# A decoder trunk on one core: one room 64 bytes longer, banks by name, output weights split in two

## Chip, cores and metric

The kernel runs on one NeuronCore of a Trainium2 chip. The metric is the device time of one execution in microseconds (us). Before the change it is 1954.59 us, the median of three runs (1953.89 to 1954.96). In the views the engines are called PE (TensorE matmul), PEld (TensorE weight load), DVE (VectorE), ACT (ScalarE), POOL (GpSimd) and SP (SyncE, which issues most DMAs).

## What is computed

A trunk of two layers on 1024 tokens of width 1024, in float32. Cut to what matters:

```python
for i in range(2):
    h = rmsnorm(x, norm_mixer[i])
    mix = short_conv_mixer(h, ...) if i == 0 else swa_sink_attention(h, ...)
    x = x + mix
    h = rmsnorm(x, norm_ffn[i])
    g, u = split(h @ w_gate_up[i])        # 1024 x 5632
    x = x + (silu(g) * u) @ w_down[i]     # 2816 x 1024
```

The attention has 16 query heads and 4 key and value heads of 64, a window of 128 tokens worked off in blocks of 128, a distance bias, a sink column in the softmax, and a norm of queries and keys per head. Its output goes through an output matrix `attn_w_o` (1024 x 1024), which the kernel calls `w_o`.

## The kernel before

**Precision.** Each matrix product is made of three float32r products: every operand is split into a high part (a rounding copy) and a low part (what the copy left over), and high x high, high x low and low x high are added in a PSUM bank. A weight block of 128 x 128 so gives three matmuls of 512 columns. For a channel mixer granule these are L918, L919 and L921, for the output matrix L1025, L1026 and L1027, for the projections to queries, keys and values L1590, L1591 and L1592, and for the first products of the convolution L157 and L161. The split is a copy on ScalarE (L857, `act.copy`) and a subtraction on VectorE (L858).

**Schemes of seven products.** The big products (gate, up and down, and most of the convolution's input product) are done by a scheme of seven products instead of eight (`sums_of`, `KINDS = 7`), in granules of up to four weight blocks (`ring_granule`). A granule's split weights go to a room of a ring of eight rooms with the tags G0 to G7, the next one free each time; 13 us (`LEAD`) before the matmuls are due, its copy is placed.

**Order.** All work from the convolution's end on is written out by a planner, `Line`. `line.work(n, f)` appends n matmuls to TensorE's order and moves the planned time on by n x `MM` = n x 0.2265 us; `line.at(t, f)` places other engines' work at a planned time. Nothing waits for a planned time: it only sets the order in which each engine, and each DMA queue, gets its instructions; each engine then works them off in order, as fast as its operands come.

**Rooms.** SBUF rooms are given out by tag with `slot`, in the order of the first request: the constants, XS0 to XS7 and A0 to A5 (8,192 bytes in each partition), two each of WR, WH and WL (4,096), then G0 to G11 (4,096 each, but G2, which has 32 bytes more, because attention lays two sets of 4 x 129 exponents in it), s0 and s1 (2,048), X0 to X7 (4,096) and small ones. PSUM has eight banks: four with the tags acc0 to acc3 and P0 to P3. A tag's next user waits until the last one's readers are done.

**Attention** (`attention_layer`). Its lead-in (L1917 and on) has three parts that matter here:

- Projections. `kv_piece(b, k)` and `q_piece(m, k)` add the k-th of eight steps of the key and value product of token block b, and of one half of the query product of block m // 2. A product's bank comes from `product_bank`, which goes round P0, P1, P2 in the order of first use. Readers of a key and value bank are `kv_v_hi`, `kv_v_lo`, `kv_square` and, last, `kv_scale` (L1683); of a query bank `q_square` and, last, `q_scale` (L1747).
- Units u = 0 to 31, one for each block and group of heads, some 6.7 us each in the plan: `scores` (L1797), then on VectorE `merge` (L1807), `bias` (L1814) and `least` (L1827), on ScalarE `exponents` (L1833), on GpSimd `normal` (L1842); a unit later `turn` (L1848, TensorE transposes the weights), `turn_hi`, `turn_lo`, `select` (L1864, GpSimd); two units later `values` (L1883). In between TensorE gets pieces of projections from `fill`, one (`next_piece`) ahead of `turn` and five behind. `key_turn` (L1696) and `q_turn` (L1762) transpose keys and queries into bank P3; `key_hi` and `key_lo` (L1700 on ScalarE, L1705 on VectorE) read the one, `q_keep` (L1767, ScalarE) the other. `q_lo` (L1756) and `o_lo` (L1914) are work of GpSimd.
- From unit 24 on the pieces are those of the output product for the first half of the tokens (`tail_piece`, `tail_part`, `tail_item`), 64 of them: eight weight tiles m of eight steps. Two more rounds, u = 32 and 33, finish the last turn and the last values, and what is left of the 64 follows. `tail_weights(m, t)` places the work for tile m, due at t: the load (L113) at t - 14.0, the copy of all 1024 columns on ScalarE at t - 5.2, the subtraction on VectorE at t - 4.2. Tile m adds up in bank P0 or P1 (`m % 2`), and is added to X on VectorE (L1050) and squared on ScalarE (L1042, L1048).

The same `tail_weights` serves the first layer and the second half of the tokens.

Of the kernel before, what the change touches and what calls it, by code (L numbers as in the profile page):

```python
# [13 lines left out]
ALU = mybir.AluOpType  # L14

P = 128
D = 1024
# [52 lines left out]
def trunk_kernel(ctx: ExitStack, tc: tile.TileContext, xT, small, table, w_in, w_out, w_kv, w_q, w_o, w_gu, w_dn, out):  # L70
# [7 lines left out]
    def slot(tag, shape=(P, D), dtype=F32, bufs=1):  # L78
        uid[0] += 1
        return sb.tile(list(shape), dtype, tag=tag, name=f"{tag}_{uid[0]}", bufs=bufs)  # L80
# [11 lines left out]
    def plain(ap):  # L92
        return ap.bitcast(F32)
# [111 lines left out]
    for tag in ("WR", "WH", "WL"):  # L205
        slot(tag, bufs=2)
    for tag in [f"G{k}" for k in range(12)]:
        slot(tag, (P, D + 8) if tag == "G2" else (P, D))
    for tag in ("s0", "s1"):
        slot(tag, (P, HALF))  # L210
    X = [slot(f"X{k}") for k in range(NK)]
# [766 lines left out]
    def channel_mixer(layer, next_stage, src_of, operands, raw_tags, extra_tags, slots, line, lead_in):  # L978
# [9 lines left out]
        ring_granule, bank_at = tools.ring_granule, tools.bank_at  # L988


        def tail_weights(m, t):
            it = {}
            c = slice(0, n_op * P)

            def load():
                it["w"] = Weights()
                it["w"].load(src_of(m), 0, n_op)

            def hi():
                it["w"].alloc()  # L1000
                it["steps"] = split_steps(it["w"].hi[:, c], it["w"].lo[:, c], it["w"].raw[:, c])
                it["steps"][0]()

            at(t - 14.0, load)
            at(t - 5.2, hi)
            at(t - 4.2, lambda: it["steps"][1]())
            return lambda: (it["w"].hi, it["w"].lo)

        tails = {}
# [1 line left out]
        def tail_part(h, m, ks):  # L1011

            c = slice(h * HALF, h * HALF + HALF)
            if (h, m) not in tails:
                tag = f"P{m % 2}" if layer and h == 0 else "acc"
                tails[h, m] = tail_weights(m, line.end), bank_at(("tail", h, m), "x", tag)
            w, get = tails[h, m]
            for k in ks:

                def three(k=k):  # L1020
                    hi, lo = w()
                    xs = operands[k]
                    ps = get()
                    kc = slice(k * P, (k + 1) * P)
                    pe.matmul(ps, hi[:, kc], xs[:, 0, c], start=k == 0, stop=False, skip_group_check=True)  # L1025
                    pe.matmul(ps, hi[:, kc], xs[:, 1, c], start=False, stop=False, skip_group_check=True)  # L1026
                    pe.matmul(ps, lo[:, kc], xs[:, 0, c], start=False, stop=k == n_op - 1, skip_group_check=True)  # L1027

                line.work(3, three)
# [455 lines left out]
    def attention_layer(line, mixer):  # L1485
        at = line.at
        xs = mixer.xs
        end0 = line.end
        small_mm = 0.42
        small_turn = 0.42  # L1490

# [81 lines left out]


        kv_ps, q_ps = {}, {}
        product_tags = deque(("P0", "P1", "P2"))

        def product_bank():
            tag = product_tags.popleft()
            product_tags.append(tag)  # L1580
            return bank(tag)

        def piece(ps_of, b, k, w):

            def three():
# [7 lines left out]

            line.work(3, three)

        def get_bank(d, key):
            def get():
                if key not in d:
                    d[key] = product_bank()
                return d[key]  # L1600

            return get

        def kv_piece(b, k):
            piece(get_bank(kv_ps, b), b, k, lambda: (WKV[k][:, 0], WKV[k][:, 1]))

        def q_piece(m, k):
            c = slice((m % 2) * HALF, (m % 2 + 1) * HALF)
            piece(get_bank(q_ps, m), m // 2, k, lambda: (WQ[k][0][:, c], WQ[k][1][:, c]))


        def mean_rows(d, b, n):
# [77 lines left out]
        KT = {}  # L1690

        def key_turn(b, c):
            ps = KT[b, c] = bank("P3")
            for g in (0, 1):
                k = kd_room()[:, 2 * c + g].rearrange("p e d -> p (e d)")
                pe.transpose(ps[:, g * P : (g + 1) * P], k, ident)  # L1696
# [59 lines left out]
            pool.tensor_tensor(s[:, :, 1, :], QC[m]["q"], s[:, :, 0, :], ALU.subtract)  # L1756

        def q_turn(m, g):
            ps = QC[m]["ps"] = bank("P3")
            s = QC[m]["split"]  # L1760
            for i in range(QUAD):
                pe.transpose(ps[:, i * P : (i + 1) * P], s[:, QUAD * g + i].rearrange("p e d -> p (e d)"), ident)  # L1762
# [5 lines left out]


        S = {}  # L1770
        sc_tags = [acc_tags[0], acc_tags[1]]
        pt_tag, pv_tag = acc_tags[2], acc_tags[3]
        NU = 2 * 2 * NB

        def parts(u):
# [2 lines left out]

        def e_room(u):
            if "E" not in room:  # L1780
                room["E"] = slot("G2", (P, D + 8))[:, 0 : 2 * QUAD * (P + 1)].rearrange(
                    "p (i h c) -> p i h c", i=2, h=QUAD
                )
            return room["E"][:, u % 2]
# [132 lines left out]
        def lead_in(tail_part, tail_item):  # L1917
# [78 lines left out]
            def unit(u, last):  # L1996

                s = line.end
                begins.append(s)
                n, g = u // 2, u % 2  # L2000
                b, c = n // 2, n % 2
                todo = deque(fill[u] if u < NU else [])

                def next_piece():
                    if todo:
                        f, *args = todo.popleft()
                        f(*args)
                    elif u >= NU:
                        tail_piece()

                if u < NU:
                    line.work(8 * (small_mm + (0.12 if b else 0.0)), scores, u)
                    e = line.end
                    at(s + 0.3, sink, u)
                    for j in (0, 1):
                        if b:
                            at(e + 0.05 + 0.85 * j, merge, u, j)
                        at(e + 0.5 + 0.85 * j, bias, u, j)
                    if b == 0:
                        at(e + 1.5, blank, u)  # L2020
                    at(e + 1.8, least, u)
                    at(e + 2.65, exponents, u)
                    at(e + 4.75, inverse, u)
                    at(e + 5.0, normal, u)
                    if g == 0:
                        kb = (b, 1) if c == 0 else (b + 1, 0)
                        if 0 < kb[0] < NB:
                            turn_keys(*kb, e + 0.3, e + 2.4)
                if 0 <= u - 2 < NU:
                    pb = (u - 2) // 4  # L2030
                    line.work(4 if pb else 2, values, u - 2)
                    at(line.end + 0.05, o_copy, u - 2)
                    at(max(line.end + 0.7, s + 3.6), o_add, u - 2)
                    if g == 1:
                        at(s + 6.95, o_hi, n - 1)
                        at(s + 7.9, o_lo, n - 1)
                next_piece()
                if 0 <= u - 1 < NU:
                    line.work(4 * small_turn, turn, u - 1)
                    at(line.end + 0.05, turn_hi, u - 1)  # L2040
                    at(max(line.end + 0.7, s + 4.2), turn_lo, u - 1)
                    if u - 1 >= 4:
                        at(line.end + 0.75, select, u - 1, 0)
                        at(max(line.end + 1.4, s + 4.95), select, u - 1, 1)
                if u >= NU:
                    for _ in range(6):
                        next_piece()
                    return
                for i in range(5):
                    next_piece()  # L2050
                    if i == (1 if g == 0 else 0) and n + 1 < 16:
                        turn_query(n + 1, g, s + 5.8)
                if n + 2 < 16 and g == 0:
                    m = n + 2
                    for d, f in (
                        (5.75, q_square),
                        (6.35, q_sum),
                        (7.2, q_guess),
                        (6.8 + 3.4, q_newton),
                        (6.8 + 5.2, q_scale),  # L2060
                        (6.8 + 6.2, q_hi),
                        (6.8 + 7.3, q_lo),
                    ):
                        at(s + d, f, m)
                if g == 1 and n < 12 and n % 2:
                    kb = n // 2 + 2
                    for d, f in (
                        (3.57, kv_v_hi),
                        (5.0, kv_v_lo),
                        (5.7, kv_square),  # L2070
                        (6.1, kv_sum),
                        (6.9, kv_guess),
                        (6.8 + 3.5, kv_scale),
                    ):
                        at(s + d, f, kb)
                if g == 0 and c == 1 and b + 1 < NB:
                    at(s + 3.5, dv_sum, b + 1)
                    at(s + 8.0, dv_hi, b + 1)
                    at(s + 8.4, dv_lo, b + 1)
# [129 lines left out]
```

## Time and profile before

| | |
|---|---|
| median of 3 runs | 1954.59 us (1953.89 to 1954.96) |
| the profiled execution | 1954.33 us, its span 1952.6 us |
| mean granted TensorE clock | 0.999 |
| instructions in the span | 24622 |
| HBM traffic | 228.76 MB read, 94.90 MB written |

Where the stages lie in the span: the first products of the convolution up to 52 us, the convolution in granules to about 241, the first layer's output product to 334, its channel mixer to about 975, attention with the first half of its output product from 978 to 1261, the second half to 1306, the second channel mixer to the end.

How to read the views: a row of the timeline is the start in us from the span's start, the duration, engine, line, operation, tiles written and read (buffer numbers left out, so G3 and G7 are both G), shapes and count; in brackets is the engine's idle time before it and what ended that. Durations of matmuls overlap and their ends are modelled; the distance between two starts is the pace. A row of waits is: who waited, for what, us in total, how often, the longest.

### The profile page before, as it was taken

The page shows a single profiled execution, that of the slowest core. Times are in us where ns is not written, and L with a number is a line of the kernel's source. Part 1 is how long each engine was busy: PE and PEld are TensorE (multiplying, and loading weights), DVE is VectorE, ACT ScalarE, POOL GpSimd, SP SyncE. Part 2 cuts the span into 40 slices and gives each one's busy share as a digit, 9 for nine tenths or more (in the row PEclk, how much of TensorE's full clock was granted, in tenths as well). Part 3 has the DMA queues.
Part 4 walks back from the last instruction along what each step waited for, and adds up shares of the span by engine and source line. Part 5 has one row for each costly group of instructions (what it writes and reads, how often), then busy time and mean ns, then how long its engine had stood idle before and what let it go on. Part 6 is the DMA issues. An engine that isn't in the chain of part 4 may idle for free.

```text
span 1952.6 us, 24622 instructions
## 1 busy us (share of the span) xinstructions
PE 1935.1 (99%) x8681; PEld 1580.7 (81%) x8681; DVE 1384.0 (71%) x2357; ACT 855.7 (44%) x1703; POOL 280.6 (14%) x442
## 2 busy tenths in 40 slices
PE   9999999999999999999999998999999999999999
PEld 7888888888888888888888887787888888888887
DVE  8997777876676767665768878678767776765543
ACT  5543444533333334444656766546333333344441
POOL 0000011011111111000025665400111111110000
PEclk9999999999999999999999999999999999999999
DMA  8522185245545537986710003433445554487562
GB/s 314 164 97 81 60 296 199 73 153 185 183 168 198 178 125 275 342 296 211 231 53 1 1 23 130 141 118 119 164 162 171 204 173 168 153 280 257 196 222 99
DMA packets 146764, 325.28 MB, mean 167 GB/s; under 512 B 14288, under 2 KB 54352, under 8 KB 146512
## 3 DMA queue, kind: packets, MB, share of 16 engines
q1 hardware_dynamic: 122592, 239.26, 36.2%
q0 software_dynamic: 23904, 84.42, 12.0%
q8 instruction: 68, 1.11, 0.2%
q14 instruction: 56, 0.46, 0.1%
q10 hardware_dynamic: 144, 0.03, 0.0%
HBM read 228.76 MB, written 94.90 MB: 166 GB/s over the span
## 4 chain that ended last, share of the span: by engine, by line
PE 94%; DVE 3%; ACT 1%; issue 1%; POOL 0%; DMA 0%; SPq 0%; DVEq 0%; POOLq 0%; ACTq 0%
PE acc L921 16%; PE acc L918 16%; PE acc L919 16%; PE P L921 9%; PE P L918 9%; PE P L919 9%; PE acc L1027 2%; PE acc L1025 2%; PE acc L1026 2%; PE P L1590 2%; PE P L1592 2%; PE P L1591 2%; PE acc L1797 1%; PE acc L157 1%; PE acc L1883 1%
## 5 line engine op out<-in xcount | busy, mean ns | idle before, releaser
L921 PE MATMUL acc<-XS,G 128*128 128x512 f32 x880 | 346.6, 394 | 0.0
L918 PE MATMUL acc<-XS,G 128*128 128x512 f32 x880 | 346.1, 393 | 0.0
L919 PE MATMUL acc<-XS,G 128*128 128x512 f32 x880 | 345.9, 393 | 0.0
L919 PEld LDWEIGHTS acc<-XS,G 128*128 128x128 f32 x880 | 165.3, 188 | 38.5
L921 PEld LDWEIGHTS acc<-XS,G 128*128 128x128 f32 x880 | 165.2, 188 | 38.0
L918 PEld LDWEIGHTS acc<-XS,G 128*128 128x128 f32 x880 | 165.3, 188 | 37.9
L918 PE MATMUL P<-A,G 128*128 128x512 f32 x476 | 187.1, 393 | 0.6 <-DVE G L1234 0.6
L921 PE MATMUL P<-A,G 128*128 128x512 f32 x476 | 187.4, 394 | 0.0
L919 PE MATMUL P<-A,G 128*128 128x512 f32 x476 | 187.0, 393 | 0.0
L921 PE MATMUL acc<-A,G 128*128 128x512 f32 x440 | 173.4, 394 | 0.0
L918 PE MATMUL acc<-A,G 128*128 128x512 f32 x440 | 173.2, 394 | 0.0
L919 PE MATMUL acc<-A,G 128*128 128x512 f32 x440 | 173.0, 393 | 0.0
L858 DVE TENSOR_TENSOR G<-WL,G 128x512 fp32r<-128x512 f32 x168 | 114.9, 685 | 56.6 <-ACT G L857 56.6
L857 ACT CAST G<-WR 128x512 fp32r<-128x512 f32 (+1 forms) x200 | 121.0, 605 | 67.1 <-PE acc L921 36.8
L858 DVE TENSOR_TENSOR G<-WR,G 128x512 fp32r<-128x512 f32 (+1 forms) x200 | 133.3, 666 | 12.0 <-ACT G L857 11.2
L857 ACT CAST G<-WH 128x512 fp32r<-128x512 f32 (+1 forms) x158 | 94.8, 600 | 87.3 <-PE acc L921 46.5
L1196 ACT ACTIVATE G<-G 128x512 f32<-128x512 f32 x88 | 55.7, 633 | 165.9 <-DVE G L1267 161.8
L921 PE MATMUL P<-XS,G 128*128 128x512 f32 x316 | 124.4, 394 | 0.0
L919 PE MATMUL P<-XS,G 128*128 128x512 f32 x316 | 124.2, 393 | 0.0
L918 PE MATMUL P<-XS,G 128*128 128x512 f32 x316 | 124.2, 393 | 0.0
L857 ACT CAST G<-WL 128x512 fp32r<-128x512 f32 x168 | 103.5, 616 | 36.0 <-DVE WL L801 31.9
L858 DVE TENSOR_TENSOR G<-WH,G 128x512 fp32r<-128x512 f32 (+1 forms) x158 | 104.4, 661 | 5.4 <-ACT G L857 5.1
(297 smaller groups left out, 3837.4 us busy)
## 6 DMA issues: line engine op xcount, KB each, us to landing
G<-h SPq DMA_DIRECT2D x70, 512.0 KB, 5.1
h<-X POOLq DMA_DIRECT2D x44, 512.0 KB, 5.2
X<-in_w_dn SPq DMA_DIRECT2D x80, 256.0 KB, 3.4
s<-X POOLq DMA_DIRECT2D x40, 512.0 KB, 4.7
WR<-in_w_gu SPq DMA_DIRECT2D x36, 512.0 KB, 6.0
WH<-in_w_gu SPq DMA_DIRECT2D x36, 512.0 KB, 6.2
h<-X POOLq DMA_DIRECT2D x66, 256.0 KB, 3.9
WR<-s SPq DMA_DIRECT2D x54, 256.0 KB, 3.3
```

Of the source, the lines that this page charges most:

```text
L857: lambda: act.copy(out_hi, raw),
L858: lambda: lo_eng.tensor_tensor(out_lo, raw, plain(out_hi), ALU.subtract),
L918: pe.matmul(ps, w[:, 0, c], x[:, 0, :], start=start and e == 0, stop=False, skip_group_check=True)
L919: pe.matmul(ps, w[:, 0, c], x[:, 1, :], start=False, stop=False, skip_group_check=True)
L921: pe.matmul(ps, w[:, 1, c], x[:, 0, :], start=False, stop=last, skip_group_check=True)
L1025: pe.matmul(ps, hi[:, kc], xs[:, 0, c], start=k == 0, stop=False, skip_group_check=True)
L1026: pe.matmul(ps, hi[:, kc], xs[:, 1, c], start=False, stop=False, skip_group_check=True)
L1027: pe.matmul(ps, lo[:, kc], xs[:, 0, c], start=False, stop=k == n_op - 1, skip_group_check=True)
L1196: state["silu"] = act.activation(x, x, AF.Silu)
L1590: pe.matmul(ps, x[:, 0, t], hi, start=k == 0, stop=False)
L1591: pe.matmul(ps, x[:, 0, t], lo, start=False, stop=False)
L1592: pe.matmul(ps, x[:, 1, t], hi, start=False, stop=k == NK - 1)
```

## The change

Four edits, none of which changes a number that is computed:

- The room G2 is 64 bytes longer than 4,096 instead of 32 (in the two places that name its shape). The exponents use as much of it as before.
- Banks of projections are assigned by name: key and value products of block b get P0 or P1 by `b % 2`, even query products P2, odd ones P0 or P1 by `m // 2 % 2`. The second key turn of the lead-in (b = 0, c = 1) gets the bank of `values`, the second query turn (m = 0, g = 1) the bank of `turn`, both among the acc banks, instead of P3. The tails of the first half take P0, P2, P1 in turn.
- For layer 1, first half, tiles 0 to 4 (`early`), the load, the copy on ScalarE and the subtraction are placed earlier, at t - 17.0, t - 8.2, and the subtraction in two pieces of 512 columns at t - 5.6 and t - 3.9.
- In round u = 32 three pieces go ahead of the last turn instead of one.

```diff
-        slot(tag, (P, D + 8) if tag == "G2" else (P, D))
+        slot(tag, (P, D + 16) if tag == "G2" else (P, D))
...
-        def tail_weights(m, t):
+        def tail_weights(h, m, t):
             it = {}
             c = slice(0, n_op * P)
+            early = layer == 1 and h == 0 and m < 5
...
+            def lo(i):
+                h = slice(i * n_op * P // 2, (i + 1) * n_op * P // 2)
+                w = it["w"]
+                dve.tensor_tensor(w.lo[:, h], w.raw[:, h], plain(w.hi)[:, h], ALU.subtract)
+
-            at(t - 14.0, load)
-            at(t - 5.2, hi)
-            at(t - 4.2, lambda: it["steps"][1]())
+            at(t - (17.0 if early else 14.0), load)
+            at(t - (8.2 if early else 5.2), hi)
+            if early:
+                at(t - 5.6, lo, 0)
+                at(t - 3.9, lo, 1)
+            else:
+                at(t - 4.2, lambda: it["steps"][1]())
...
-                tag = f"P{m % 2}" if layer and h == 0 else "acc"
-                tails[h, m] = tail_weights(m, line.end), bank_at(("tail", h, m), "x", tag)
+                tag = ("P0", "P2", "P1")[m % 3] if layer and h == 0 else "acc"
+                tails[h, m] = tail_weights(h, m, line.end), bank_at(("tail", h, m), "x", tag)
...
-            piece(get_bank(kv_ps, b), b, k, lambda: (WKV[k][:, 0], WKV[k][:, 1]))
+            piece(get_bank(kv_ps, b, f"P{b % 2}"), b, k, lambda: (WKV[k][:, 0], WKV[k][:, 1]))
...
-            piece(get_bank(q_ps, m), m // 2, k, lambda: (WQ[k][0][:, c], WQ[k][1][:, c]))
+            piece(get_bank(q_ps, m, f"P{m // 2 % 2}" if m % 2 else "P2"), m // 2, k, lambda: (WQ[k][0][:, c], WQ[k][1][:, c]))
...
-            ps = KT[b, c] = bank("P3")
+            ps = KT[b, c] = bank(pv_tag if b == 0 and c else "P3")
...
-            ps = QC[m]["ps"] = bank("P3")
+            ps = QC[m]["ps"] = bank(pt_tag if m == 0 and g else "P3")
...
-                next_piece()
+                for _ in range(3 if u == NU else 1):
+                    next_piece()
                 if 0 <= u - 1 < NU:
                     line.work(4 * small_turn, turn, u - 1)
```

Left out are the removal of `product_bank`, the tag that `get_bank` now takes, the two lines that name the banks earlier in the function, and the second place that names G2's shape.

More of the change, by code (lines that the diff above doesn't have):

```diff
@@ L1488, in attention_layer @@
         end0 = line.end
+        sc_tags = [acc_tags[0], acc_tags[1]]
+        pt_tag, pv_tag = acc_tags[2], acc_tags[3]
         small_mm = 0.42
@@ L1575, in attention_layer @@
         kv_ps, q_ps = {}, {}
[L1576 to L1581, printed above, removed]
         def piece(ps_of, b, k, w):
@@ L1594, in piece, with get_bank @@
             line.work(3, three)
-        def get_bank(d, key):
+        def get_bank(d, key, tag):
             def get():
                 if key not in d:
-                    d[key] = product_bank()
+                    d[key] = bank(tag)
                 return d[key]
@@ L1770, in attention_layer @@
         S = {}
-        sc_tags = [acc_tags[0], acc_tags[1]]
-        pt_tag, pv_tag = acc_tags[2], acc_tags[3]
         NU = 2 * 2 * NB
@@ L1780, in e_room @@
             if "E" not in room:
-                room["E"] = slot("G2", (P, D + 8))[:, 0 : 2 * QUAD * (P + 1)].rearrange(
+                room["E"] = slot("G2", (P, D + 16))[:, 0 : 2 * QUAD * (P + 1)].rearrange(
                     "p (i h c) -> p i h c", i=2, h=QUAD
```

## The prediction

> **What bounds the kernel now.** I read the page first, then the list of TensorE's waits, then its timeline in the long stages. The page gives the profiled execution's span and says how much of it TensorE leaves unused.
>
> ```profile
> span 1952.6 us, 24622 instructions
> PE 1935.1 (99%) x8681; PEld 1580.7 (81%) x8681; DVE 1384.0 (71%) x2357; ACT 855.7 (44%) x1703; POOL 280.6 (14%) x442
> ```
>
> TensorE is idle for 17.5 us of 1952.6. So the time can fall in two ways only: the idle time goes, or the matmuls come at a quicker pace. The waits of TensorE between 965 and 1300 us, which holds attention and so nearly all lines of the diff, are these (waiting line, releaser, us in total, times, longest):
>
> ```profile
> PE P L1762 <- DVE G L1705: 4.7, 1, 4.7
> PE P L1762 <- DVE at_t L1625: 1.8, 1, 1.8
> PE acc L1848 <- POOL G L1842: 1.4, 1, 1.4
> PE P L1590 <- DVE G L1683: 1.3, 1, 1.3
> PE P L1696 <- ACT G L1767: 1.2, 2, 0.7
> PE P L1696 <- DVE G L1705: 0.4, 1, 0.4
> PE P L1762 <- ACT G L1767: 0.3, 1, 0.3
> ```
>
> That is 11.1 us in eight stops. The long stretches around them have next to none, as a row below shows for one, so there the pace decides. The timeline of TensorE in the first channel mixer shows it; these are the first matmuls of granules (12 matmuls each: four blocks, three products), with the granules between them left out:
>
> ```profile
> 700.16 0.39 PE L918 MATMUL acc<-XS,G 128*128 128x512 f32 x1
> ...
> 702.89 0.39 PE L918 MATMUL acc<-XS,G 128*128 128x512 f32 x1
> ...
> 711.28 0.39 PE L918 MATMUL acc<-XS,G 128*128 128x512 f32 x1
> ...
> 722.33 0.39 PE L918 MATMUL acc<-XS,G 128*128 128x512 f32 x1
> ```
>
> The first granule takes 2.73 us, the next three 8.39, 2.80 each; eight, one turn of the ring, take 22.17 us. With q short granules and 8 - q long ones that gives q = (8 x 2.797 - 22.17) / 0.067 = 3.1, so three short and five long. The ring has eight rooms, and exactly five of them (G3 to G7) are allocated behind the one long room G2, three (G0 to G2) up to it. Matmuls whose weights lie in the rooms ahead of G2 altogether run like this:
>
> ```profile
> 1252.05 0.39 PE L1025 MATMUL P<-XS,WH 128*128 128x512 f32 x1
> ...
> 1262.25 0.39 PE L1025 MATMUL acc<-XS,WH 128*128 128x512 f32 x1
> ```
>
> Between these two rows lie 45 matmuls in 10.20 us, 0.2267 us each. The ring's mean is 22.17 / 96 = 0.2309, its long granules' 8.39 / 36 = 0.2331.
>
> **The longer room.** The change lengthens G2 by another 32 bytes, moves all rooms behind it (G3 to G11, s0, s1, X0 to X7) by as much, and adds no instruction. Every room between the constants and G2 is a multiple of 4,096 bytes long, so all of those start at one common residue; the rooms behind it start 32 bytes past that residue now, and 64 past it after. The view by source line (count: shortest/median/longest ns) helps to tell content from place: the same kind of product with weights from XS (ahead) or from G (a mixture).
>
> ```profile
> L918 PE MATMUL acc<-XS,G x880: 387/395/476, 97.5 to 1945.9; 128*128 128x512 f32 x176
> L918 PE MATMUL P<-A,G x476: 387/395/467, 64.3 to 1932.7; 128*128 128x512 f32 x159
> L918 PE MATMUL acc<-A,G x440: 387/395/478, 53.2 to 1948.0; 128*128 128x512 f32 x147
> L918 PE MATMUL P<-XS,G x316: 387/395/396, 75.4 to 1930.6; 128*128 128x512 f32 x158
> L918 PE MATMUL acc<-XS,XS x16: 389/389/389, 359.4 to 369.6; 128*128 128x512 f32 x16
> L157 PE MATMUL acc<-XS,G x32: 395/396/396, 42.0 to 52.5; 128*128 128x512 f32 x32
> ```
>
> Weights in XS never take longer than 389 ns, and in the convolution's first products (rooms G6 to G10, all behind G2) never less than 395. I take it that a weight room off a 64-byte boundary costs, and that the new length puts all of them on one. The sum: L918, L919 and L921 each issue 880 + 476 + 440 + 316 = 2112 of these matmuls, 6336 together; (0.2309 - 0.2267) us each is 0.00427 with one more digit, so 27.1 us. As a check from the long granules alone: 5/8 of 6336 is 3960, times 0.0064, is 25.3. The convolution's 32 shown are part of some 100 there, 0.6 us. In attention the moving operand can lie in such a room too: four of the eight query weights are in X rooms.
>
> ```profile
> L1590 PE MATMUL P<-A,XS x80: 389/389/481, 987.7 to 1187.4; 128*128 128x512 f32 x80
> L1590 PE MATMUL P<-X,XS x64: 393/400/483, 993.1 to 1194.5; 128*128 128x512 f32 x64
> ```
>
> At 5 to 11 ns for 192 matmuls that is 1 to 2 us; scores and values, which also read G rooms, aren't shown on a boundary, so between 0 and 2. I take 1.5 for both. Together 29.2 us.
>
> Nothing hides this gain: TensorE waits for nobody there, and the other engines keep pace. This is the stretch with the busiest VectorE (length, then busy time of TensorE, weight loads, VectorE, ScalarE, GpSimd):
>
> ```profile
> 50.00:240.00 190.00, 190.00 (x824) 154.44 (x823) 162.69 (x252) 83.50 (x147) 0.92 (x2) 1.00 0.29 98
> ```
>
> TensorE is busy for all of 190.00 us, VectorE for 162.69, ScalarE for 83.50. The due times are also written for 0.2265 us a matmul (MM), so a quicker TensorE only reaches the pace for which the rest is placed.
>
> The Trainium skill speaks against this edit: "TensorE: Matmul & The Clock Gate", section "Back-to-back issue gap", makes the gap N/2.4 + 2.5 ns, 216 ns at 512 columns, wherever the weights lie, and by it the pad gives nothing. The trace has two paces for one N (227 and 233 ns), so I follow the rows; the page's case is the first rival.
>
> **Banks by name.** Key and value products now alternate between P0 and P1, even query products take P2, odd ones P0 and P1. In the fourth row of the waits, L1590 waits for L1683, the last reader of the previous key and value product in the bank that the rotation gives it: 1.3 us. With the next one in the other bank, the bank's last user is a query product whose scaling is due some 5 us before that of the key product (12.0 behind a turn that begins 6.7 earlier, against 10.3). The second key turn and the second query turn of the lead-in take banks that attention doesn't need yet: their rows, 0.4 and 0.3, go. Gain 2.0. The two L1696 waits for L1767 (1.2) aren't touched.
>
> **Output weights split earlier and in two pieces.** This aims at the two largest waits. VectorE ahead of the first of them:
>
> ```profile
> 1207.56 3.64 DVE L858 TENSOR_TENSOR WL<-WR,WH 128x1024 fp32r<-128x1024 f32 x1 [2.04 <-ACT WH L857]
> ...
> 1213.03 0.47 DVE L1705 SCALAR_TENSOR_TENSOR G<-P,qkg,G 128x256 fp32r<-128x256 f32 x1
> ```
>
> One subtraction takes 3.64 us, after 2.04 us of waiting for ScalarE's copy, and L1705, which frees the bank for L1762, stands behind it. GpSimd at that time:
>
> ```profile
> 1206.59 1.28 POOL L1756 TENSOR_TENSOR G<-s,G 128x512 f32<-128x512 f32 x1
> 1207.83 1.69 POOL L1914 TENSOR_TENSOR XS<-s,XS 128x128 fp32r<-128x128 f32 x4
> 1209.49 0.62 POOL L1864 TENSOR_SCALAR_AFFINE_SELECT G<-G 128x512 fp32r<-128x512 f32 x1
> ```
>
> VectorE finishes 1.1 us after GpSimd's last one ends at 1210.11. The same shape at 1176.10, with a wait of 1.55 us ahead of it, is behind the wait of 1.8:
>
> ```profile
> 1176.10 1.46 DVE L858 TENSOR_TENSOR WL<-WR,WH 128x1024 fp32r<-128x1024 f32 x1 [1.55 <-ACT WH L857]
> ```
>
> With the copy due 3 us earlier, VectorE no longer waits 2.04 and 1.55 us for it, and half the subtraction is done 1.4 us before it stood there. The first wait also leaves matmuls at half pace behind it:
>
> ```profile
> 1214.39 0.78 PE L1025 MATMUL P<-XS,WH 128*128 128x512 f32 x1
> ...
> 1216.65 0.40 PE L1027 MATMUL P<-XS,WL 128*128 128x512 f32 x1
> ```
>
> Five matmuls take 2.26 us between these starts instead of 1.13. So 4.7 + 1.8 + 1.1 = 7.6 us are to be had. What comes in their place: the second half can still meet GpSimd's stretch (I leave 1.2 us of wait for that, half of the 3.64 - 1.46 = 2.2 us of blocking, rounded up); and ScalarE's copy now stands ahead of L1767, which frees the bank for the next L1696:
>
> ```profile
> 1206.47 1.05 ACT L857 CAST WH<-WR 128x1024 fp32r<-128x1024 f32 x1
> ```
>
> That delays L1767 by between 0 and 1.05 us; I take 0.5, nearer to neither end, since the work ahead of it also comes earlier. Gain 7.6 - 1.2 - 0.5 = 5.9. The loads move 3 us ahead on SyncE's queue; they wait for the same rooms as now, and what stands behind them, the reload of X, is wanted much later: nothing.
>
> On the lock the Trainium skill says ("SBUF — State Buffer", section "Who interferes with whom") that a VectorE instruction with two SBUF inputs is shut out by a GpSimd one for that whole instruction. By that alone two halves are two chances to be shut out, each up to 1.28 us, and together no shorter than the 3.64 now: the 4.7 and 1.1 would stay, and the sum would end at 1922. The trace differs from the page: the wait went over six GpSimd instructions in a row, not one, so what counts is being ahead of the row.
>
> **More pieces ahead of the last turn.** L1848 waits 1.4 us for L1842. Two more pieces are six matmuls, 6 x 0.2267 = 1.36 us, taken from behind the turn: gain 1.4.
>
> **The sum.** 29.2 + 2.0 + 5.9 + 1.4 = 38.5 us. The profiled execution took 1954.33 us, 1.7 more than its span and 0.3 less than the median, so I take 38.5 from the median: 1916.
>
> **Rivals.**
> *The pad does nothing.* The two paces then come from what shares the time with a granule, not from its place, and only the 9.3 us of waits go: 1945. For it: buffer numbers aren't in the rows, so no row names a costly room. Against: three to five is the split of the rooms, and 389 against 395 shows in two stages, once with all rooms of a group behind G2. The page on the gap is on this side. 6%. If, with it, new stops eat the 9.3, the time stays at 1955: 2%.
> *The stops move instead of going.* The copy ahead of L1767 and two shut-out halves cost what the edits win; the pad's 29.2 remain: 1925. For it: VectorE is in order, and one blocked half delays the same L1705. 13%.
> *VectorE becomes the bound from 50 to 240 us.* It is busy 162.69 of 190; TensorE's gain there is 3.5 us (824 x 0.00427) and would be lost: 1920. Against: even 186 us leave it 24. 6%.
> *Slower: the distance counts, not the boundary.* If the price grows with the distance from the common residue, it is 12.8 ns at 64 bytes, and the 29.2 us are added instead: 1955 + 29.2 - 9.3 = 1974. It decides from 2.4 ns more for a matmul of a long granule (9.3 us / 3960). Against: nothing in the trace has such a distance. 3%.
>
> **How the numbers follow.** My forecast has 70%, its own range is 1911 (all of 12.2 us of waits and stalls, 4 us in attention: 1954.6 - 43.9) to 1921 (half of the waits' 9.3 stay). Up to 1928 the range takes in the second and third rivals, the second with 3 us of spread; left out are the cases at 1945, 1955 and 1974. Faster by over 0.2% (3.9 us, about what a measurement of this kernel can tell from no change): 0.70 + 0.13 + 0.06 + 0.06 = 0.95; same 0.02; slower 0.03.
>
> **What would show it.** L918, L919 and L921 with G at a median of 389 instead of 395, and 2.72 us for every granule: the pad is right. At 395, the first rival; above 400, the last. L1590 on X at 389 to 392. No L1762 after L1705 and no L1590 after L1683 in the waits, L858 on WL at 512 columns near 0.7 us ten times, no 0.63 us matmuls: the rest is right. An L1696 waiting over 1 us for L1767 shows the third rival's copy. If TensorE's idle time grew anywhere between 50 and 960 us, I'd be wrong about the cover.

## The result and the profile after

After the change the kernel takes 1951.88 us, the median of 20 runs (1950.41 to 1952.85); before takes 1954.78 beside it (20 runs, 1953.86 to 1955.94). The ratio is 0.9985, with a 95% interval from 0.9978 to 0.9992: 2.9 us are won where 38.5 were forecast, and the time lies outside the range. The profiled execution took 1951.75 us. Its page, first the span and instructions, then the busy time of the engines:

```profile
span 1950.0 us, 24687 instructions
...
PE 1937.1 (99%) x8681; PEld 1581.5 (81%) x8681; DVE 1389.9 (71%) x2362; ACT 855.8 (44%) x1703; POOL 282.5 (14%) x442
```

TensorE is idle for 12.9 us instead of 17.5, yet busy for 2 us more: stops have gone, and the matmuls have not become quicker. These are all of TensorE's waits between 965 and 1300 us (waiting line, releaser, us in total, times, longest):

```profile
PE P L1767 <- DVE G L1710: 5.1, 2, 3.6
PE P L1701 <- ACT G L1772: 1.0, 2, 0.8
```

Some lines have new numbers: L1767 is the query turn, before L1762; L1710 was L1705, L1701 was L1696, L1772 was L1767. Eight stops of 11.1 us have become four of 6.1. The stops behind L1683 and ahead of the last turn and the lead-in's turns are gone; the one that the split aimed at is still 3.6 us long.

The timeline of TensorE in the first channel mixer shows what became of the pace. These are the first matmuls of eight granules and of the ninth, with the matmuls between them left out:

```profile
701.26 0.39 PE L918 MATMUL acc<-XS,G 128*128 128x512 f32 x1
...
703.98 0.40 PE L918 MATMUL acc<-XS,G 128*128 128x512 f32 x1
...
706.78 0.40 PE L918 MATMUL P<-A,G 128*128 128x512 f32 x1
...
709.58 0.40 PE L918 MATMUL P<-XS,G 128*128 128x512 f32 x1
...
712.38 0.39 PE L918 MATMUL acc<-XS,G 128*128 128x512 f32 x1
...
715.13 0.40 PE L918 MATMUL P<-A,G 128*128 128x512 f32 x1
...
717.93 0.40 PE L918 MATMUL acc<-A,G 128*128 128x512 f32 x1
...
720.73 0.39 PE L918 MATMUL acc<-XS,G 128*128 128x512 f32 x1
...
723.48 0.39 PE L918 MATMUL acc<-XS,G 128*128 128x512 f32 x1
```

The distances are 2.72, 2.80, 2.80, 2.80, 2.75, 2.80, 2.80, 2.75: three short granules and five long ones, as before, and a short one behind a long one now takes 2.75. One turn of the ring is 22.22 us instead of 22.17. The view by source line has the same (count, shortest/median/longest ns); the median is 393 where 395 was before and 389 was expected.

```profile
L918 PE MATMUL acc<-XS,G x880: 389/393/482, 97.7 to 1943.3; 128*128 128x512 f32 x176
```

So two things are open: why 64 bytes leave the five rooms as dear as 32 did, and why the subtraction's two halves leave a stop of 3.6 us. The theory on the first, formed from this profile, was that what counts is where a weight room starts against where the *moving* operand starts (XS and A, at the common residue), whatever boundary either of them is on. Its rivals: a boundary coarser than 64 bytes that the weights alone must be on; and that the place does not matter.

### The profile page after: what moved, and what is told of

Read it like the earlier page. It is cut to its first block, busy times and chain, and to the rows that moved or that the text cites. A ratio compares the mean times of both kernels' runs of the same rounds, so it can differ in the third digit from the quotient of the medians.

```text
span 1950.0 us, 24687 instructions
## 1 busy us (share of the span) xinstructions
PE 1937.1 (99%) x8681; PEld 1581.5 (81%) x8681; DVE 1389.9 (71%) x2362; ACT 855.8 (44%) x1703; POOL 282.5 (14%) x442
## 4 chain that ended last, share of the span: by engine, by line
PE 94%; DVE 3%; POOL 1%; issue 1%; ACT 0%; DMA 0%; SPq 0%; POOLq 0%; DVEq 0%
PE acc L921 16%; PE acc L919 16%; PE acc L918 16%; PE P L919 9%; PE P L918 9%; PE P L921 9%; PE acc L1037 2%; PE acc L1035 2%; PE acc L1036 2%; PE P L1597 2%; PE P L1595 2%; PE P L1596 2%; PE acc L1800 1%; PE acc L1886 1%; PE acc L157 1%
## 5 line engine op out<-in xcount | busy, mean ns | idle before, releaser
L921 PE MATMUL acc<-XS,G 128*128 128x512 f32 x880 | 346.5, 394 | 0.0
L919 PE MATMUL acc<-XS,G 128*128 128x512 f32 x880 | 346.5, 394 | 0.0
L918 PE MATMUL acc<-XS,G 128*128 128x512 f32 x880 | 346.4, 394 | 0.0
L919 PEld LDWEIGHTS acc<-XS,G 128*128 128x128 f32 x880 | 165.3, 188 | 38.4
L918 PEld LDWEIGHTS acc<-XS,G 128*128 128x128 f32 x880 | 165.4, 188 | 38.2
L921 PEld LDWEIGHTS acc<-XS,G 128*128 128x128 f32 x880 | 165.3, 188 | 38.2
L918 PE MATMUL P<-A,G 128*128 128x512 f32 x476 | 187.2, 393 | 0.6 <-DVE G L1244 0.6
L921 PE MATMUL P<-A,G 128*128 128x512 f32 x476 | 187.3, 394 | 0.0
L919 PE MATMUL P<-A,G 128*128 128x512 f32 x476 | 187.3, 394 | 0.0
L918 PE MATMUL acc<-A,G 128*128 128x512 f32 x440 | 173.4, 394 | 0.0
L921 PE MATMUL acc<-A,G 128*128 128x512 f32 x440 | 173.2, 394 | 0.0
L919 PE MATMUL acc<-A,G 128*128 128x512 f32 x440 | 173.2, 394 | 0.0
L921 PE MATMUL P<-XS,G 128*128 128x512 f32 x316 | 124.4, 394 | 0.0
L919 PE MATMUL P<-XS,G 128*128 128x512 f32 x316 | 124.3, 393 | 0.0
L918 PE MATMUL P<-XS,G 128*128 128x512 f32 x316 | 124.3, 393 | 0.0
```

What stands on the lines that cost most here:

```text
L918: pe.matmul(ps, w[:, 0, c], x[:, 0, :], start=start and e == 0, stop=False, skip_group_check=True)
L919: pe.matmul(ps, w[:, 0, c], x[:, 1, :], start=False, stop=False, skip_group_check=True)
L921: pe.matmul(ps, w[:, 1, c], x[:, 0, :], start=False, stop=last, skip_group_check=True)
```

## The experiments: the place of the rooms

**The long room at the end.** Everything in the ring then starts at the common residue, with the room's length unchanged.

```diff
-        slot(tag, (P, D + 16) if tag == "G2" else (P, D))
+        if tag != "G2":
+            slot(tag)
...
     X = [slot(f"X{k}") for k in range(NK)]
+    slot("G2", (P, D + 16))
```

> The changed kernel with the long room G2 given out behind X7, so that no other room stands off the common residue; everything else stays. In the changed kernel G3 to G7 still take 233 ns a matmul and G0 to G2 227. Residue theory (the price comes from a start off the common residue, by 64 bytes as by 32): every ring granule takes 2.72 us, L918, L919 and L921 have a median of 389 ns, time 1951.9 - 29 = 1923 us. Place theory (rooms that start above about 154,000 bytes cost, whatever their residue): G3 moves down 4,160 bytes and becomes short, G2 becomes long, the others stay, so the granules are three short to five long as before, time 1950 to 1953. Content theory (what runs beside a granule sets its pace): nothing changes, 1952.

Measured: 1922.02 us (4 runs), ratio 0.9831 (0.9815 to 0.9847). In its view by source line L918 stands as L920:

```profile
L920 PE MATMUL acc<-XS,G x880: 389/389/486, 96.6 to 1913.4; 128*128 128x512 f32 x176
```

With the common residue the whole price goes, 29.9 us against after. The place matters.

**Other lengths.** In both lines that give G2's shape, `D + 16` becomes `D + 32` (128 bytes), `D + 64` (256) or `D + 128` (512).

> The changed kernel with G2 128 bytes longer than 4,096 instead of 64. If what counts is a start off a 128-byte step from the common residue: all ring granules 2.72 us, 1923 us. If the step is longer than 128 bytes, or if the place or the content counts: three short and five long granules as before, 1950 to 1953 us.

> The changed kernel with G2 256 bytes longer than 4,096. At 128 bytes a matmul of a long granule took 232.6 ns, at 512 none was long. If the step that counts is 512 bytes: still long, 230 to 233 ns, 1938 to 1950 us. If it is 256 bytes: all granules 2.72 us, 1921 us.

> The changed kernel with G2 512 bytes longer than 4,096. If the step that counts is 512 bytes or less: all ring granules 2.72 us, 1923 us. If it is longer (up to 4,096), or if the place or the content counts: 1950 to 1953 us.

Measured: 1945.08 us with 128 bytes (2 runs, 0.995, 0.993 to 0.997), 1922.41 with 256 (2 runs, 0.9833, 0.9813 to 0.9852), 1920.47 with 512 (2 runs, 0.9824, 0.9804 to 0.9844). The same view of TensorE's timeline with 128 bytes, four granules of it, the first short and three long:

```profile
699.22 0.39 PE L918 MATMUL acc<-XS,G 128*128 128x512 f32 x1
...
701.95 0.40 PE L918 MATMUL acc<-XS,G 128*128 128x512 f32 x1
...
710.31 0.39 PE L918 MATMUL acc<-XS,G 128*128 128x512 f32 x1
```

2.73 us for the first, 8.36 for the next three: 8.36 / 36 = 0.2322 us a matmul (0.2326 over all five long granules of a turn of the ring), still dear. With 256 bytes the start of a granule and of the second one after it are these:

```profile
700.93 0.39 PE L918 MATMUL acc<-XS,G 128*128 128x512 f32 x1
...
706.37 0.39 PE L918 MATMUL acc<-A,G 128*128 128x512 f32 x1
```

5.44 us for 24 matmuls, 0.2267 each, and with 512 the same. So of the lengths tried, 256 and 512 bytes are free of the price; 32, 64 and 128 are not. The time with 128 bytes is below the 1950 to 1953 us expected for dear rooms: the granules are a little cheaper, and the stops in attention come to 4.1 us there instead of 6.1.

**All rooms moved together.** The constants, which come first, are made 64 bytes longer. Each room's place changes; no distance between rooms does.

```diff
-    cst = slot("cst", (P, C_END))
+    cst = slot("cst", (P, C_END + 16))[:, 0:C_END]
```

> The changed kernel with the constants 64 bytes longer, so that every room, ahead of G2 and behind it, starts 64 bytes later; the distance between the two kinds stays 64. If the distance between weights and moving operand counts: as the changed kernel, 1950 to 1953 us. If an absolute step of 128 bytes counts, the two kinds change places: the weights in G0 to G2, WH and WL take 233 ns a matmul and those in G3 to G7 227, time about 1952 - 27 + 16 = 1941 us. Place or content theory: 1950 to 1953 us.

Measured: 1952.05 us (8 runs), 0.9983 (0.9973 to 0.9994), after's own time.

```profile
L918 PE MATMUL acc<-XS,G x880: 389/393/482, 97.8 to 1944.4; 128*128 128x512 f32 x176
```

The median is still 393, with three short granules and five long ones, and the output weights, which lie ahead of G2, still run at 227 ns a matmul. A boundary that the weights alone must be on would have changed which rooms are dear; a distance would not.

**The moving operands moved.** XS and A are put 64 bytes later, and a second gap behind them makes up the rest of 512 bytes. So G3 to G7 now stand as XS and A do, while G0 to G2, WR, WH and WL stand 64 bytes ahead of them (both modulo 512).

```diff
-    cst = slot("cst", (P, C_END))
+    cst = slot("cst", (P, C_END + 16))[:, 0:C_END]
...
         pair_slot(tag)
+    slot("gap", (P, 112))
```

> The changed kernel with XS0 to XS7 and A0 to A5 (moving operands) 64 bytes later against WR, WH, WL, G0, G1 and G2, so that they stand as G3 to G11 and X stand. Distance theory: the two kinds of rooms change places. A matmul with weights in G3 to G7 takes 227 ns, in G0 to G2, WH and WL 233; the ring has five short and three long granules, the output weights' matmuls a start-to-start of 233 ns; time about 1952 - 27 + 16 + 5 = 1946 us. Rival (what counts is where the weights lie by themselves): three short and five long granules as in the changed kernel, output weights at 227 ns, 1950 to 1953 us.

Measured: 1929.95 us (2 runs), 0.9871 (0.9851 to 0.9891). Its timeline (L919 is after's L918):

```profile
701.18 0.39 PE L919 MATMUL P<-XS,G 128*128 128x512 f32 x1
...
703.90 0.39 PE L919 MATMUL acc<-XS,G 128*128 128x512 f32 x1
...
706.65 0.39 PE L919 MATMUL P<-A,G 128*128 128x512 f32 x1
...
712.09 0.39 PE L919 MATMUL acc<-XS,G 128*128 128x512 f32 x1
...
717.58 0.39 PE L919 MATMUL P<-A,G 128*128 128x512 f32 x1
...
723.02 0.39 PE L919 MATMUL acc<-XS,G 128*128 128x512 f32 x1
```

From 701.18 the granules take 2.72 and 2.75 us, then two 5.44, two 5.49, two 5.44: short, long, short, short, long, long, short, short. Read round the ring from the sixth on, that is long, three short, long, two short, long, where after has short, three long, short, two long, short. The kinds have changed places. The output weights in WH and WL, cheap in after, have become dear with G0 to G2; this is the end of the first half's output product:

```profile
1238.26 0.40 PE L1036 MATMUL P<-XS,WH 128*128 128x512 f32 x1
...
1243.86 0.40 PE L1036 MATMUL P<-XS,WH 128*128 128x512 f32 x1
```

That is 24 matmuls in 5.60 us, 233.3 ns each, as expected for them. That settles the theory: the distance to the moving operand decides whether there is a price. A size was missed: the three rooms of the ring cost 2.745 / 12 = 228.8 ns a matmul and not 233. For 3/8 of 6336 matmuls that is some 10 of the 16 us by which the time lies below the 1946 expected; some 3 more are the price of the five rooms, 29.9 with the room last and not 27. In the second half of the output product, with weights in the same WH and WL, it is some 229 ns again. One distance so has two prices, and the distance alone doesn't fix the size.

**The pad alone, and with the room that it needs.** The kernel before, with only G2's shape changed, to `D + 16` and to `D + 128`.

> The kernel before with the longer room alone (64 bytes over 4,096 instead of 32). Distance theory (a weight room pays wherever its start is off the moving operand's by something other than a multiple of 512 bytes): the five rooms pay as before, at 64 bytes slightly more (233.4 instead of 233.1 ns a matmul, and half of the next granule too), so plus 1 to 2.5 us: ratio 1.0005 to 1.0013. Rival, that the pad itself is neutral or a small gain and the 3 us come from it: ratio 0.9985 to 1.0000.

> The kernel before with G2 512 bytes longer than 4,096, and nothing else. The prediction's price of long granules, 27.1 us in the ring, 0.6 in the convolution and 0 to 4 in attention, is right if it is saved whole: 1955 - 28 = 1927 us, ratio 0.985 to 0.986. If part of it is lost to waits of attention, whose order stays: up to 1931 us.

Measured: 1956.92 us with 64 bytes (11 runs), 1.0009 (1.0000 to 1.0018), against 1955.31 for before; 1927.39 with 512 (4 runs), 0.9858 (0.9842 to 0.9875), against 1955.26. The 64 bytes cost 1.6 us, at the edge of what the interval tells from no change; their granules are those of after, with 2.75 us for a short one behind a long one. The right distance brings 27.9, with before's waits in attention still there.

```profile
L918 PE MATMUL acc<-XS,G x880: 388/390/486, 96.4 to 1918.9; 128*128 128x512 f32 x176
```

## The experiments: the stops

**The rest alone.** After, with the pad back at `D + 8`.

> The changed kernel with the room back at 32 bytes over 4,096: banks by name, two pieces, more pieces ahead of the last turn. If the pad costs 1.9 us in the changed kernel and the rest wins the stops that are gone from the list of waits (1.4, 1.3, 0.4 and part of the 4.7): minus 4 to 6 us, ratio 0.9970 to 0.9980. If the rest wins only the 3 us of the whole change: ratio 0.9985.

Measured: 1946.87 us (5 runs), 0.9958 (0.9945 to 0.9970), 8.4 won, more than the 4 to 6 expected. Its waits in the same stretch:

```profile
PE P L1767 <- DVE G L1710: 3.6, 2, 3.0
PE P L1701 <- ACT G L1772: 0.7, 1, 0.7
```

These are 4.3 us instead of 11.1. So the 64 bytes cost 5.0 us in the changed kernel and 1.6 in the one before: some of that is in the stops. The longest stop comes in two sizes over the runs: 3.6 us (and 1.5 for the other) in after and in the kernels with the room at the end, with 256 bytes, with longer constants and with the moved operands; 2.9 to 3.0 (and 0.5 to 0.6) here and with 128 and 512 bytes. What decides between them was not followed up; the edits are worth some us more or less by it.

The timeline of VectorE in after, ahead of that stop (L1008 is the half subtraction, L1810 and L1817 prepare scores, L1710 frees the bank):

```profile
1204.10 1.95 DVE L1008 TENSOR_TENSOR WL<-WR,WH 128x512 fp32r<-128x512 f32 x1
...
1206.49 0.43 DVE L1817 TENSOR_TENSOR G<-acc,A 128x256 f32<-128x256 f32 x1
1206.83 3.32 DVE L1008 TENSOR_TENSOR WL<-WR,WH 128x512 fp32r<-128x512 f32 x1
...
1211.59 0.48 DVE L1710 SCALAR_TENSOR_TENSOR G<-P,qkg,G 128x256 fp32r<-128x256 f32 x1
```

And GpSimd beside it:

```profile
1206.06 1.29 POOL L1761 TENSOR_TENSOR G<-s,G 128x512 f32<-128x512 f32 x1
1207.31 1.71 POOL L1917 TENSOR_TENSOR XS<-s,XS 128x128 fp32r<-128x128 f32 x4
1208.98 0.63 POOL L1867 TENSOR_SCALAR_AFFINE_SELECT G<-G 128x512 fp32r<-128x512 f32 x1
```

The second half begins 0.77 us into GpSimd's row of six instructions and ends at 1210.15, 0.54 after the row: 2.6 us of its 3.32 are waiting. Three more operations then stand ahead of L1710.

A row of that kind need not be waited out, though. In the same kernel the second half for an earlier tile meets the same six instructions at the same point:

```profile
1176.45 1.06 DVE L1008 TENSOR_TENSOR WL<-WR,WH 128x512 fp32r<-128x512 f32 x1
...
1175.68 1.29 POOL L1761 TENSOR_TENSOR G<-s,G 128x512 f32<-128x512 f32 x1
1176.93 2.15 POOL L1917 TENSOR_TENSOR XS<-s,XS 128x128 fp32r<-128x128 f32 x4
```

It too begins 0.77 us into the row, but it is done 0.54 us after the first of the six ends, and L1917's four take 2.15 us instead of 1.71: here GpSimd waits for the half. The first half at 1204.10 is also let in between two GpSimd instructions, after 1.27 us of waiting. What decides who waits was not found.

The long stop also leaves matmuls at half pace behind it, at a granted clock of 0.50 between 1213 and 1215 us:

```profile
1212.91 0.56 PE L1036 MATMUL P<-XS,WH 128*128 128x512 f32 x1
...
1215.83 0.63 PE L1037 MATMUL P<-XS,WL 128*128 128x512 f32 x1
```

Seven intervals take 2.92 us instead of 1.59. Two kernels change who meets whom there.

**The second half later**, behind the operations that lead to L1710:

```diff
-                at(t - 3.9, lo, 1)
+                at(t - 1.5, lo, 1)
```

> The changed kernel with the second half of the subtraction due at t - 1.5 instead of t - 3.9, behind the work that frees the bank for the query turn. Lock theory (a subtraction of two SBUF operands stands still while GpSimd works without a gap, and what is behind it waits too): at its new place GpSimd has gaps, each second half takes 0.7 to 1.3 us, the stop of 3.6 us at the query turn of unit 28 falls below 1 and the matmuls at half pace behind it go: 1952 - 4 = 1948 us. Rival (VectorE simply has too much to do there, so something else is late in its place): a stop of at least 2.5 us stays, 1950 to 1952 us.

Measured: 1948.83 us (6 runs), 0.9968 (0.9956 to 0.9980). VectorE's timeline:

```profile
1206.75 0.43 DVE L1817 TENSOR_TENSOR G<-acc,A 128x256 f32<-128x256 f32 x1
1207.09 0.42 DVE L1810 COPY_PREDICATED acc<-cst,acc 128x256 f32<-128x256 int32 x1
...
1208.61 0.47 DVE L1710 SCALAR_TENSOR_TENSOR G<-P,qkg,G 128x256 fp32r<-128x256 f32 x1
...
1209.73 0.68 DVE L1008 TENSOR_TENSOR WL<-WR,WH 128x512 fp32r<-128x512 f32 x1
```

GpSimd's row is the same as in after, 0.25 us later:

```profile
1207.55 1.71 POOL L1917 TENSOR_TENSOR XS<-s,XS 128x128 fp32r<-128x128 f32 x4
1209.23 0.63 POOL L1867 TENSOR_SCALAR_AFFINE_SELECT G<-G 128x512 fp32r<-128x512 f32 x1
```

The operations with an input in PSUM take 0.42 to 0.47 us right beside the row; the half, now at the row's end, takes 0.68. L1710 comes 3 us earlier, the longest stop behind it is 0.5 us, the half-paced matmuls are gone. That the half stood ahead of L1710 is thus what made the long stop; how long a half waits beside GpSimd isn't settled by it. In return L1772 is late by 0.5 us more, and what L1886 reads is late three times, by 0.8 together:

```profile
PE P L1701 <- ACT G L1772: 1.5, 2, 0.8
PE P L1767 <- DVE G L1710: 0.9, 2, 0.5
PE acc L1886 <- POOL G L1867: 0.5, 2, 0.3
PE acc L1886 <- DVE G L1863: 0.3, 1, 0.3
```

**GpSimd's part of the row later.** `o_lo` (L1917) is due 2 us later, so the low part of the attention's output may be read from a room that other work has rewritten.

```diff
-                        at(s + 7.9, o_lo, n - 1)
+                        at(s + 9.9, o_lo, n - 1)
```

> The changed kernel with GpSimd's split of the attention output (four instructions) due 2 us later in each odd unit; VectorE's order stays. Lock theory: the second half at about 1206.8 us meets one GpSimd instruction instead of a row of six, takes at most 1.5 us instead of 3.32, and the stop at the query turn falls from 3.6 to 1.8 or less. Rival (too much work): it still takes over 3 us or the stop stays over 3.

Measured: 1952.92 us (8 runs), 0.9989 (0.9979 to 0.9999), and nothing learned of the row: GpSimd is behind its plan there and has L1761, L1917 and L1867 in the same sequence as in after, so the half meets the same row.

```profile
1207.19 3.32 DVE L1008 TENSOR_TENSOR WL<-WR,WH 128x512 fp32r<-128x512 f32 x1
```

**Both cures.** After, with 512 bytes and the second half at t - 1.5.

> Two findings together: the changed kernel with G2 512 bytes longer than 4,096 and the second half of the subtraction due at t - 1.5. If they add up: 1920.5 (the 512 bytes alone) less the stop at the query turn of unit 28 with the matmuls at half pace behind it (2.9 + 1.1 us), so 1916 to 1918 us. If TensorE, now quicker, only runs into the next late step of VectorE or ScalarE: 1919 to 1921 us.

Measured: 1915.82 us (4 runs, 1915.79 to 1916.39), 0.980 (0.9785 to 0.9814): 39.4 us below before, as if the two add up, and the best of all kernels here.

## Why the prediction was wrong, point by point

- **The longer room: wrong, and this is the step that failed.** "I take it that a weight room off a 64-byte boundary costs, and that the new length puts all of them on one." The rows of before show two paces, and they show that the rooms behind G2 are the dear ones; they hold one distance only, 32 bytes, and say nothing of the step. No row gives 64; it is the length in the change. What counts is the distance to the moving operand: at 64 bytes the matmuls of a long granule still take 233.3 ns each, at 0, 256 and 512 bytes 226.7. The pad alone gave +1.6 us where -29.2 stood. The reading behind it was right: five rooms of eight, and a price of 27.9 us where 29.2 was worked out. (One figure in it was read too widely: with weights in XS, L918 never takes longer than 389 ns, but L921 takes up to 397.) Its 1.5 for attention is not borne out: with the room last, L1590's successor still has a median of 397 ns on both A and X, as after.
- **Banks by name: right.** The waits of 1.3, 0.4 and 0.3 us are gone: 2.0.
- **The last turn: right.** The 1.4 is gone.
- **The split: mechanism right, size wrong.** 1.2 us were left for the second half's meeting with GpSimd. It met a row of six and waited for all of it, which the half for an earlier tile, at the same point of the same row, did not have to: the stop fell from 4.7 to 3.6 only, its half-paced matmuls cost 1.3 instead of 1.1, the other stop fell from 1.8 to 1.5. With L1701's 1.2 fallen to 1.0 that is 1.4 instead of 5.9. The 0.5 charged for the copy ahead of L1772 did not show in after; it does (1.5 instead of 1.0) once the longer stop is gone.
- **The sum by what was measured:** -1.6 + 2.0 + 1.4 + 1.4 = 3.2 us, against 2.9. The two failures, 30.8 and 4.5, are the whole distance from 38.5. That the kernel did get faster, as forecast, is the work of the other edits against the pad.
- **The cover: right.** With the quick pace the other engines kept up; the kernels with it win 28 to 33 us over the same ones without, so VectorE does not become the bound.
- **The rivals.** The last one, given 3%, had the mechanism, distance (from the residue at which XS and A start) and not boundary, with the wrong law: a price that grows with the distance, where the price is nearly flat from 32 to 128 bytes and gone at 256. The result lies between the first rival's two times, 1945 and 1955, but not for its reason: the place matters, only 64 bytes don't mend it.

## What to carry to other kernels

A row that shows two paces shows that a place has a price; it doesn't show which step is free of it, so take the distance to zero (or try several) before counting on a size. Keep the starts of stationary and moving operands alike, here modulo 256 bytes, or put an odd-sized room behind all of them. Of a VectorE subtraction with both inputs in SBUF, ask what GpSimd does in the whole stretch around it: it may get in after one instruction or only after the last. So place it behind what frees a bank.

## What was not expected of the hardware

The pace of matmuls of 512 columns by the start of the weight room less that of the moving operand:

| bytes | 0 | 32 | 64 | 128 | 256 | 512 | -64 |
|---|---|---|---|---|---|---|---|
| ns | 226.7 | 233.1 | 233.3 | 232.2 | 226.7 | 226.7 | 228.8 or 233.3 |

At -64 the lower figure is that of the ring and the higher that of the output weights in WH and WL towards the end of the first half, so a second thing sets the size; what it is was not followed up. That there is a price wherever the distance is no multiple of 256 fits all these values; 192 and other steps were not tried. At 64 bytes the price runs on into the next granule (2.75 us instead of 2.72); before's turn of 22.17 us leaves hardly any room for that at 32. Which resource the two share stays open. The Trainium skill ("TensorE: Matmul & The Clock Gate", section "Step-by-step: what each phase is for") gives the stream and the weight load a read port each, by which loading takes nothing from a running matmul; here the place of the one against the other changes the pace by 6.6 ns, so in time they are not independent.

A VectorE subtraction with two SBUF inputs waited 2.6 us, until a row of six GpSimd instructions was over, while operations with one input in PSUM ran beside the same row in 0.42 to 0.47 us. The second is what the Trainium skill says ("SBUF — State Buffer", section "Who interferes with whom"); the first goes beyond the one instruction that it names. It is not a rule either: a like subtraction, as far into a like row, waited 0.4 us, for one instruction alone.
